# Closer lags in an attention pipeline that runs beside a weight stream: transposes five slots and values six behind the scores, rotations in halves, heads split two units ahead

## The chip, the cores and the metric

The kernel runs on one core of one Trainium2 chip. The metric is the device time of one execution in microseconds (us); where several runs are given, it is their median. Five engines work side by side, each with its own instruction list in a fixed order: TensorE (PE in the profile, its weight loads PEld), VectorE (DVE), ScalarE (ACT), GpSimd (POOL) and SyncE (SP, which here only issues DMAs). An instruction waits for semaphores of other engines, and everything behind it on its engine waits too.

## The reference, cut to what matters

One trunk layer for 512 tokens of width 2048, all in float32. An input projection feeds two mixers side by side, their outputs are normalised per group and projected back, and a SwiGLU block follows.

```
h = rmsnorm(x, g_mix)
qa, ka, va, qb, kb, vb = split(h @ w_in)            # 8 heads of q, 2 of k and v (A); 8 heads each (B)
# mixer A: grouped queries, all 512 keys
q = axial_rope(rmsnorm(qa, g_q)) * HD**-0.5;  k = axial_rope(rmsnorm(ka, g_k))
out_a = softmax(q @ k.T) @ va
# mixer B: three dilated windows (128,1), (512,4), (2048,16), merged by their softmax denominators
q = partial_rope(qb) * HD**-0.5;  k = partial_rope(kb)     # the first 32 of 128 dims are rotated
out_b = sum(wts * branch for branch in branches)
mixed = concat(rmsnorm(out_a, g_out_a), rmsnorm(out_b, g_out_b))
x = x + mixed @ w_out
gate, up = split(rmsnorm(x, g_ffn) @ w_gate_up)
x = x + (silu(gate) * up) @ w_down
out = rmsnorm(x, g_final)
```

## The kernel before

**Products.** Every float32 matrix product is made of three products of split operands: a value is divided into a high half (ACT writes it, rounded) and a low half (DVE subtracts the high half from the value). `split` (from L227) does this, `mm3` (L240 to L244) issues the three products hi x hi, hi x lo, lo x hi, so each full product shows as L242, L243, L244. The two lines of `split` without a gain are L233 (ACT) and L234 (DVE), with a gain L236 and L237.

**Units.** The weights stream in tiles of 128 rows. One `Unit` is one such tile with its 12 products (three for each of four row tiles of tokens, or of four column tiles). All units lie in one list, and the loop at the end of the program goes through it. The units that matter are those of the last input projections, then eight units for each of the four output chunks of mixer A, which start at unit 216 (`out_chunk("A", c)`), and from unit 248 the same for mixer B. An output chunk multiplies the eight heads' outputs with one 512-column block of W_out and adds the result, scaled per row, to x.

**Side work.** Attention is not a stage of its own: it is a list of small tasks (`side`) taken while units run. `give` (L711) adds credit: half of it after the second row tile of a unit (`by_rows`, L728), the rest at the unit's end; a task is taken while the credit covers its cost. Between `attend[0]` and `attend[1]` a unit brings 2.8 credits, from there to `attend[2]` 1.3 (`HEAD_RATE`), after that one credit per unit end. `attend[1]` lies `ATTEND_PAST` units behind the last input projection, `attend[2]` as many behind mixer A's output chunks. Where the program needs something not yet made, `drain_until` takes tasks at once, whatever their cost: for a head's output, and in `post` (the addition to x) for the row scale `ro`.

**Slots.** A task `head_slot(s)` (L643) issues, for four slots per head and sixteen heads (0 to 7 of A, 8 to 15 of B), one step of a pipeline: the score of slot s (three products on PE, then the maximum on DVE, L573, or for B the mask and maximum in one custom operation, L577), the normalisation of slot s-1 (L591, L592), the four transposes of probabilities of slot s-`TURN_LAG` (L597, then the split into `pTh` on ACT and `pTl` on DVE), the exponential on ACT (L584, L587), and the value products of slot s-`VALUE_LAG`. After a head's last value product `fin` copies its output (L614, `oT`) and squares it (L619); `add_squares` (L626) adds the squares of the heads into `acc`. After head 7 of a mixer `row_rms` goes to the front of the side list: PE's column sums of `acc` (L387), a copy and a scaling on DVE (L389, L222), a power on POOL (L224). The addition to x in `post` is L1022 on DVE. Behind it `h_side` (L1062) transposes x for the next stage (L1068).

**Other tasks between slots.** `norm_rope` rotates and normalises queries of A (L448 to L453 for one row tile). Its second block of queries (`qA1`) is loaded by a DMA and turned while the first heads run. `rope_partial` (L522, L525, L526) rotates a row tile of a projection `qkB`, that holds queries and keys of two heads of B; two row tiles are one task. `Back` loads and splits heads that were written to DRAM. `early(k)` splits the outputs of heads that stayed in SBUF (`oS`, L236 and L237 with `oT` as source), one unit before the unit that multiplies them.

**PSUM.** There are eight banks, handed out in the order in which they were released: four are held by the chunk, one by a head's output, three go round between scores, transposes of probabilities and transposes of queries and keys.

Of the kernel before, what the change touches and what calls it, by code (L numbers as in the profile page):

```python
# [15 lines left out]
OP = mybir.AluOpType  # L16
# [3 lines left out]
P = 128  # L20
# [3 lines left out]
NT = S // P  # L24
KD = D // P
NC = D // 512
NHA, NKV, NHB = 8, 2, 8
# [5 lines left out]
PARTIAL = HD // 4  # L33
# [21 lines left out]
EARLY = 2  # L55
EVICT = 6
HEAD_RATE = (2.8, 1.3)
TURN_LAG = 6
VALUE_LAG = 8
COLUMN_BLOCKS = 3  # L60
SUM_LEAD = 6
ATTEND_PAST = 6


def f32(ap):
# [4 lines left out]
def encoder_block(ctx, tc, x, g_mix, w_in, g_q_a, g_k_a, g_out_a, g_out_b, w_out, g_ffn,  # L70
                  w_gate_up, w_down, g_final, c_ident, c_mask, c_axial, c_partial, out):
    nc = tc.nc
# [13 lines left out]
    def slot(base, dtype=F32, shape=(P, 512)):  # L86
        return sp.tile(list(shape), dtype, tag="s", name=nm(base))
# [19 lines left out]
    def small(n=4):  # L107
        used[0] += n
        assert used[0] <= 512
        return smalls[:, used[0] - n:used[0]]  # L110
# [32 lines left out]
    turning = cp.tile([P, 512], F32, name="turning")  # L143
# [3 lines left out]
    ropeb = fixed[:, 256:512].rearrange("p (a t c) -> p a t c", a=2, t=NT)  # L147
# [72 lines left out]
    def rsqrt_mean(ss, n, count):  # L220
        t = small(n)
        nc.vector.tensor_scalar(t, ss, 1.0 / count, EPS, op0=OP.mult, op1=OP.add)  # L222
        r = small(n)
        nc.gpsimd.tensor_tensor(r, t, mhalf[:, :n], op=OP.pow)  # L224
        return r
# [23 lines left out]
    units = []  # L249
# [176 lines left out]
    def norm_rope(get, nh, name):  # L426
        w = nh * HD
        st = {}

        def squares(t):  # L430
            if t == 0:
                st["ss"] = small(NT * nh)
            junk, q0 = slot("rj"), get(t)[0]
            for h in range(nh):
                nc.scalar.activation(junk[:, h * HD:(h + 1) * HD], q0[:, h * HD:(h + 1) * HD], AF.Square,
                                     accum_out=st["ss"][:, nh * t + h:nh * t + h + 1])
            if t == NT - 1:
                st["rs"] = rsqrt_mean(st["ss"], NT * nh, HD)

        def turned(t):  # L440
            q0, dst = get(t)
            gc, gs = tabs[name]
            tmp = slot("ra")
            q4 = q0.rearrange("p (h a s d) -> p h a s d", h=nh, a=2, s=2)
            t4 = tmp[:, :w].rearrange("p (h a s d) -> p h a s d", h=nh, a=2, s=2)
            s4 = gs[:, t, :].rearrange("p (a s d) -> p a s d", a=2, s=2)
            for s in range(2):
                nc.vector.tensor_tensor(t4[:, :, :, s, :], q4[:, :, :, 1 - s, :],  # L448
                                        s4[:, None, :, s, :].to_broadcast([P, nh, 2, 32]), op=OP.mult)
            q3 = q0.rearrange("p (h d) -> p h d", h=nh)  # L450
            nc.vector.tensor_tensor(q3, q3, gc[:, t, :][:, None, :].to_broadcast([P, nh, HD]), op=OP.mult)
            nc.vector.tensor_tensor(q0, q0, tmp[:, :w], op=OP.add)
            nc.vector.tensor_tensor(dst.rearrange("p (h d) -> p h d", h=nh), q3,  # L453
                                    st["rs"][:, nh * t:nh * (t + 1), None].to_broadcast([P, nh, HD]), op=OP.mult)
        return [[lambda t=t, f=f: f(t) for t in range(NT)] for f in (squares, turned)]

    qA, kA, kTA, vA = {}, {}, {}, {}
    vB, qkB = {}, {}
# [20 lines left out]
    def reload(name, dst):  # L479
        assert stored[name] == NT, name  # L480
        whole = slot(name, F32, (P, NT, 512))
        nc.sync.dma_start(whole, spill[name].rearrange("t p c -> p t c"))
        dst.update((t, whole[:, t]) for t in range(NT))

    def split_vA(t):
        if not vA:
# [10 lines left out]
    def transpose_k_a(kv):  # L497
        ps = bank()
        for t in range(NT):
            nc.tensor.transpose(ps[:, t * P:(t + 1) * P], kA[t][:, 256 + kv * HD:256 + (kv + 1) * HD], ident)  # L500
        kTA[kv] = split(ps, "kT", at=((2, 4 + 2 * kv), (2, 5 + 2 * kv)))
        release(ps)
# [8 lines left out]
    def split_vB(h):  # L511
        vB[h] = split(vB[h].rearrange("p t c -> p (t c)"), "v", at=heads[NHA + h].home("v"))

    turn = [0]

    def rope_partial(q0, t):
        rot = q0.rearrange("p (h d) -> p h d", h=4)[:, :, :PARTIAL]
        turn[0] ^= 1
        tmp = turning[:, 256 + 128 * turn[0]:384 + 128 * turn[0]].rearrange("p (h c) -> p h c", h=4)
        hp = PARTIAL // 2  # L520
        for s in range(2):
            nc.vector.tensor_tensor(  # L522
                tmp[:, :, s * hp:(s + 1) * hp], rot[:, :, (1 - s) * hp:(2 - s) * hp],
                ropeb[:, 1, t, s * hp:(s + 1) * hp][:, None, :].to_broadcast([P, 4, hp]), op=OP.mult)
        nc.vector.tensor_tensor(rot, rot, ropeb[:, 0, t, :][:, None, :].to_broadcast([P, 4, PARTIAL]), op=OP.mult)  # L525
        nc.vector.tensor_tensor(rot, rot, tmp, op=OP.add)  # L526

    oT = {}
# [114 lines left out]
    def head_slot(s):  # L643
        def at(lag, f, only=None):
            head, i = head_at(s - lag)
            if head and (only is None or i == only):
                f(head, i)
        at(VALUE_LAG + 1, lambda head, i: head.add_squares(), NT - 1)
        at(0, Head.score)
        at(1, Head.norm)  # L650
        at(TURN_LAG, Head.pt)
        at(0, Head.exp)
        at(VALUE_LAG, Head.pv)
        at(VALUE_LAG, lambda head, i: head.fin(), NT - 1)
        at(-4, lambda head, i: head.tq(), 0)
# [6 lines left out]
    def light(cost, tasks):  # L662
        return [weighed(cost, f) for f in tasks]

    def attention_tasks():
        def q_tasks(j):
            return norm_rope(lambda t: (qA[j][t], qA[j][t]), 4, "q")

        def both(cost, *lists):
            return [weighed(cost, lambda fs=fs: [f() for f in fs]) for fs in zip(*lists)]  # L670

        def b_ropes(j):
            return light(0.5, [lambda t=t: (rope_partial(qkB[j][t], t), rope_partial(qkB[j][t + 1], t + 1))
                               for t in (0, 2)])
        qA.update({j: {} for j in range(2)})
        qkB.update({j: {} for j in range(4)})
        push_heads()
        k_squares, k_turned = norm_rope(lambda t: (kA[t][:, :256], kA[t][:, 256:]), NKV, "k")
        q_squares, q_turned = q_tasks(0)
        vs = [lambda t=t: split_vA(t) for t in range(NT)]  # L680
        tables = light(0.8, table_tasks())
        todo = tables[:3] + both(1.4, [lambda t=t: scale_k(t) for t in range(NT)], k_squares)
        todo += both(0.6, vs) + tables[3:]
        todo += both(2.0, q_squares, k_turned) + both(2.6, q_turned)
        todo += light(0.6, [lambda kv=kv: transpose_k_a(kv) for kv in range(NKV)]) + [heads[0].tq, heads[0].tk]
        extra = {}

        def at(slot, tasks):
            extra.setdefault(slot, []).extend(tasks)
        at(0, light(0.1, [lambda: reload("qA1", qA[1])]))  # L690
        at(20, light(0.1, [lambda: nc.sync.dma_start(mask, c_mask)]))
        for n, (cost, tasks) in enumerate(zip((1.0, 1.5), q_tasks(1))):
            for t, f in enumerate(both(cost, tasks)):
                at(3 + 4 * n + t, [f])
        for j in range(4):
            s = NT * (NHA + 2 * j)
            at(s - 11, light(0.1, [lambda j=j: reload(f"qkB{j}", qkB[j])]))
            for n, f in enumerate(b_ropes(j)):
                at(s - 8 + n, [f])
        for h in range(NHB):  # L700
            s = NT * (NHA + h)
            at(s + 2, light(0.1, [lambda h=h: load_vB(h)]))
            at(s + 4, light(0.4, [lambda h=h: split_vB(h)]))
        for s in range(2 * NHA * NT + VALUE_LAG + 2):
            cost = 1.5 if s < NHA * NT else 1.2 if s < 2 * NHA * NT else 0.7
            todo += [weighed(cost, lambda s=s: head_slot(s))] + extra.get(s, [])
        return todo
# [249 lines left out]
    todo = attention_tasks()  # L957
# [134 lines left out]
    for kind in "AB":  # L1092
        for c in range(NC):
            out_chunk(kind, c)
        if kind == "A":
            attend.append(len(units) + ATTEND_PAST)
    attend[1] += ATTEND_PAST

# [231 lines left out]
    at = [0.0]  # L1330
# [66 lines left out]
    for n, u in enumerate(units):  # L1397
        share["now"], share["due"] = n, 1.0
        if n < KD:
            if n + 5 < KD:  # L1400
                load_x(n + 5)
            if n + 1 < KD:
                x_prep(n + 1)
            if 4 < n < 10:
                next(gains, None)
        if n < KD + 8:
            row_squares(n)
        prepare(n)
        for v in units[n + 1:n + 2]:
            if v.early is not None:  # L1410
                v.early()
                v.early = None
        u.mm(u)
        if u.post is not None:
            u.post()
        for f in hooks.pop(n, ()):
            f()
        give(1.0)
# [54 lines left out]
```

## Time and profile before

| quantity | value |
|---|---|
| median of 3 runs | 1996.3 us (1996.21 to 1997.05) |
| the profiled execution | 1996.13 us |
| its span in the profile | 1994.3 us |
| mean granted TensorE clock | 0.996 |
| busy: PE, DVE, ACT, POOL | 99%, 80%, 57%, 6% |

A row of the timeline gives the start in the span, the duration, the engine, the line of the program, the operation with output<-input, and how many such instructions in a row it covers; in brackets stands the idle time of that engine just before and the engine, output and line that ended it. PE's products are pipelined: one starts some 0.23 us after the other, while each is listed with about 0.39. Names have their buffer numbers left out in the profile; the order of instructions has them. In the order, a row is one instruction (or `x4` alike) in the place that it has on its engine, without time.

### The profile page before, as it was taken

The numbers are of one execution on the slowest core, as the hardware profiler recorded it, in microseconds if no ns is written. First come the engines' busy times: TensorE is split into PE (matmuls) and PEld (weight loads), VectorE is DVE, ScalarE is ACT, GpSimd is POOL, SyncE is SP. The second block draws the span as 40 slices with busy tenths as digits, with TensorE's granted clock in tenths as the row PEclk, the third lists the DMA queues.
The fourth block names the chain that finished last, engine by engine and source line by source line (L and its number), as shares of the span: only waits on it lengthen the run. The fifth ranks groups of instructions, "written<-read, shape, count | busy, mean of one in ns | idle before, by whom it ended". The sixth has DMA issues, their size and how long they took to land. (4 is left out here: it accounts for less than half of the span.)

```text
span 1994.3 us, 27604 instructions
## 1 busy us (share of the span) xinstructions
PE 1971.8 (99%) x8972; PEld 1623.9 (81%) x8972; DVE 1594.9 (80%) x2773; ACT 1130.0 (57%) x2071; POOL 121.3 (6%) x162
## 2 busy tenths in 40 slices
PE   9999999999999999999999999999999999999998
PEld 7888888777888888888888888888888888788886
DVE  6887778887775698878878877878779887877977
ACT  7655555564555565554555555555556666666655
POOL 0100001000000000000000000000000122111121
PEclk9999999998999999999999999999999999999999
DMA  8576683143333644846737647558467698768765
GB/s 276 180 280 211 209 284 119 58 143 111 127 121 118 216 167 168 293 132 233 269 124 258 228 158 277 182 183 286 145 218 269 189 280 248 189 171 275 203 153 167
DMA packets 235874, 394.83 MB, mean 198 GB/s; under 512 B 22561, under 2 KB 77649, under 8 KB 235601
## 3 DMA queue, kind: packets, MB, share of 16 engines
q1 hardware_dynamic: 211440, 330.85, 49.1%
q0 software_dynamic: 17200, 40.38, 9.1%
q10 hardware_dynamic: 7088, 21.83, 3.1%
q8 instruction: 70, 1.15, 0.2%
q14 instruction: 76, 0.61, 0.1%
HBM read 330.33 MB, written 62.65 MB: 197 GB/s over the span
## 5 line engine op out<-in xcount | busy, mean ns | idle before, releaser
L242 PE MATMUL b<-tw,arena 128*128 128x512 f32 x2244 | 879.4, 392 | 2.4 <-ACT ev L1215 2.4
L243 PE MATMUL b<-tw,arena 128*128 128x512 f32 x2244 | 873.9, 389 | 0.8 <-DVE tw L830 0.4
L244 PE MATMUL b<-tw,arena 128*128 128x512 f32 x2244 | 874.1, 390 | 0.0
L827 ACT ACTIVATE tw<-raw 128x512 fp32r<-128x512 f32 x924 | 558.6, 628 | 430.3 <-DVE raw L871 276.5
L830 DVE TENSOR_TENSOR tw<-raw,tw 128x512 fp32r<-128x512 f32 x924 | 617.4, 685 | 167.7 <-ACT tw L827 161.4
L242 PEld LDWEIGHTS b<-tw,arena 128*128 128x128 f32 x2244 | 421.4, 188 | 89.3 <-ACT ev L1215 3.5
L243 PEld LDWEIGHTS b<-tw,arena 128*128 128x128 f32 x2244 | 421.5, 188 | 88.5 <-DVE tw L830 2.1
L244 PEld LDWEIGHTS b<-tw,arena 128*128 128x128 f32 x2244 | 421.2, 188 | 88.0
L871 DVE TENSOR_TENSOR raw<-raw,raw 128x512 f32<-128x512 f32 x528 | 360.0, 683 | 0.7 <-DMA raw<-in_w_gate_up_dram 0.6
L1216 POOL DMA_DIRECT2D x1d<-ev x76 | 66.5, 978 | 1146.8 <-ACT ev L1215 1136.7
L827 ACT ACTIVATE tw<-stage 128x512 fp32r<-128x512 f32 x140 | 85.4, 628 | 67.7 <-DVE stage L871 45.7
L830 DVE TENSOR_TENSOR tw<-stage,tw 128x512 fp32r<-128x512 f32 x140 | 93.3, 685 | 23.6 <-ACT tw L827 23.5
L242 PE MATMUL b<-w,arena 128*128 128x512 f32 x240 | 95.8, 399 | 0.0
L244 PE MATMUL b<-w,arena 128*128 128x512 f32 x240 | 93.9, 391 | 0.0
L233 ACT ACTIVATE pTh<-b 128x512 fp32r<-128x512 f32 x64 | 38.3, 599 | 97.7 <-PE b L597 94.6
L243 PE MATMUL b<-w,arena 128*128 128x512 f32 x240 | 93.5, 390 | 0.0
L365 DVE TENSOR_TENSOR pair<-pair 128x256 f32<-128x256 f32 x120 | 45.5, 420 | 26.7 <-ACT pair L1071 25.7
L1215 ACT ACTIVATE ev<-b,smalls 128x512 f32<-128x512 f32 x76 | 49.6, 682 | 27.5 <-PE b L244 26.2
L1119 DVE TENSOR_TENSOR s<-b,s 128x512 f32<-128x512 f32 x66 | 44.0, 687 | 24.8 <-PE b L244 24.8
L242 PE MATMUL b<-arena,arena 128*128 128x512 f32 x128 | 53.0, 414 | 2.0 <-ACT arena L236 2.0
L244 PE MATMUL b<-arena,arena 128*128 128x512 f32 x128 | 51.6, 403 | 2.0 <-DVE arena L237 2.0
L1147 ACT ACTIVATE pair<-b 128x512 f32<-128x512 f32 x44 | 26.3, 597 | 47.8 <-PE b L1144 47.5
(210 smaller groups left out, 1797.6 us busy)
## 6 DMA issues: line engine op xcount, KB each, us to landing
raw<-in_w_gate_up_dram SPq DMA_DIRECT2D x616, 256.0 KB, 5.3
raw<-in_w_down_dram SPq DMA_DIRECT2D x176, 256.0 KB, 7.0
stage<-in_w_in_dram SPq DMA_DIRECT2D x111, 256.0 KB, 5.0
forms<-pair SPq DMA_DIRECT2D x22, 896.0 KB, 5.3
x1d<-ev POOLq DMA_DIRECT2D x76, 256.0 KB, 6.7
fr<-forms ACTq DMA_DIRECT2D x35, 512.0 KB, 5.8
raw<-in_w_out_dram SPq DMA_DIRECT2D x32, 512.0 KB, 4.3
stage<-in_w_in_dram SPq DMA_DIRECT2D x90, 128.0 KB, 3.4
```

Source lines behind the costliest of these rows:

```text
L233: nc.scalar.activation(hi, src, AF.Copy)
L242: nc.tensor.matmul(dst, ah, bh, start=start, stop=False, skip_group_check=chained)
L243: nc.tensor.matmul(dst, ah, bl, start=False, stop=False, skip_group_check=chained)
L244: nc.tensor.matmul(dst, al, bh, start=False, stop=stop, skip_group_check=chained)
L365: nc.vector.tensor_tensor(out, x, y, op=op)
L827: nc.scalar.activation(self.pair[:, 0], self.src, AF.Copy)
L830: nc.vector.tensor_tensor(self.pair[:, 1], self.src, f32(self.pair[:, 0]), op=OP.subtract)
L871: nc.vector.tensor_tensor(t[dst], t[src[0]], t[src[1]], op=OP.add if form == "m6" else OP.subtract)
L1119: nc.vector.tensor_tensor(d[:, t], box.bank_of(form)[t], d[:, t], op=OP.add)
L1147: nc.scalar.activation(st["pair"][:, half * 1024:half * 1024 + 512], ps, AF.Copy)
L1215: nc.scalar.activation(e, box.bank_of(form)[t], AF.Copy, scale=r2["r"][:, row:row + 1])
L1216: nc.gpsimd.dma_start(x1_dram[2 * cb + j, row], e, accum_op=OP.add)
```

## The change

Six edits are made together. (1) `TURN_LAG` goes from 6 to 5 and `VALUE_LAG` from 8 to 6: transposes come five slots behind the score, the value products one slot behind the transposes in place of two; the list has two slots fewer at its end. (2) `ATTEND_PAST` goes from 6 to 4: `attend[2]` is unit 252 in place of 254, `attend[1]` 220 in place of 222. (3) `norm_rope` returns three lists: the addition of the rotated part and the scaling, until now the end of `turned`, are a task of their own, `scaled`. For the second block of queries the squares are at slots 0, 0, 1, 1, and the two halves alternate from slot 2 to 9; before, squares were at 3 to 6 and whole rotations at 7 to 10. (4) The reload of that block is the last task before slot 0 in place of the first behind it. (5) `rope_partial` rotates the four row tiles of a projection in one call of four operations, seven slots before the first head's score; before, there were two tasks of two calls, eight and seven slots ahead. (6) `early` is called for the next two units in place of the next one.

Three lines more in the program ahead of `norm_rope`'s end and fewer further down shift line numbers: L573 and L577 become L576 and L580, L591 and L592 become L594 and L595, L597 becomes L600, L626 becomes L629, L1022 becomes L1023, L1068 becomes L1069. L522, L525, L526 become L525, L528, L529.

```diff
-TURN_LAG = 6
-VALUE_LAG = 8
+TURN_LAG = 5
+VALUE_LAG = 6
...
-ATTEND_PAST = 6
+ATTEND_PAST = 4
...
             nc.vector.tensor_tensor(q3, q3, gc[:, t, :][:, None, :].to_broadcast([P, nh, HD]), op=OP.mult)
-            nc.vector.tensor_tensor(q0, q0, tmp[:, :w], op=OP.add)
+            st["tmp"] = tmp
+
+        def scaled(t):
+            q0, dst = get(t)
+            q3 = q0.rearrange("p (h d) -> p h d", h=nh)
+            nc.vector.tensor_tensor(q0, q0, st["tmp"][:, :w], op=OP.add)
             nc.vector.tensor_tensor(dst.rearrange("p (h d) -> p h d", h=nh), q3,
                                     st["rs"][:, nh * t:nh * (t + 1), None].to_broadcast([P, nh, HD]), op=OP.mult)
-        return [[lambda t=t, f=f: f(t) for t in range(NT)] for f in (squares, turned)]
+        return [[lambda t=t, f=f: f(t) for t in range(NT)] for f in (squares, turned, scaled)]
...
-    turn = [0]
-
-    def rope_partial(q0, t):
-        rot = q0.rearrange("p (h d) -> p h d", h=4)[:, :, :PARTIAL]
-        turn[0] ^= 1
-        tmp = turning[:, 256 + 128 * turn[0]:384 + 128 * turn[0]].rearrange("p (h c) -> p h c", h=4)
+    def rope_partial(q):
+        rot = q.rearrange("p t (h d) -> p t h d", h=4)[:, :, :, :PARTIAL]
+        tmp = turning.rearrange("p (t h c) -> p t h c", t=NT, h=4)
...
-        todo += both(2.0, q_squares, k_turned) + both(2.6, q_turned)
+        todo += both(2.0, q_squares, k_turned, k_scaled) + both(2.6, q_turned, q_scaled)
         todo += light(0.6, [lambda kv=kv: transpose_k_a(kv) for kv in range(NKV)]) + [heads[0].tq, heads[0].tk]
+        todo += light(0.1, [lambda: reload("qA1", qA[1])])
...
-        at(0, light(0.1, [lambda: reload("qA1", qA[1])]))
         at(20, light(0.1, [lambda: nc.sync.dma_start(mask, c_mask)]))
-        for n, (cost, tasks) in enumerate(zip((1.0, 1.5), q_tasks(1))):
-            for t, f in enumerate(both(cost, tasks)):
-                at(3 + 4 * n + t, [f])
+        q_squares, q_turned, q_scaled = q_tasks(1)
+        for t in range(NT):
+            at(t // 2, both(0.8, q_squares[t:t + 1]))
+            at(2 + 2 * t, both(0.9, q_turned[t:t + 1]))
+            at(3 + 2 * t, both(0.9, q_scaled[t:t + 1]))
         for j in range(4):
             s = NT * (NHA + 2 * j)
             at(s - 11, light(0.1, [lambda j=j: reload(f"qkB{j}", qkB[j])]))
-            for n, f in enumerate(b_ropes(j)):
-                at(s - 8 + n, [f])
+            at(s - 7, light(0.9, [lambda j=j: rope_partial(qkB[j]["whole"])]))
...
-        for v in units[n + 1:n + 2]:
+        for v in units[n + 1:n + 3]:
             if v.early is not None:
                 v.early()
                 v.early = None
```

More of the change, by code (lines that the diff above doesn't have):

```diff
@@ L483, in reload @@
         dst.update((t, whole[:, t]) for t in range(NT))
+        dst["whole"] = whole
     def split_vA(t):
@@ L522, in rope_partial @@
             nc.vector.tensor_tensor(
-                tmp[:, :, s * hp:(s + 1) * hp], rot[:, :, (1 - s) * hp:(2 - s) * hp],
-                ropeb[:, 1, t, s * hp:(s + 1) * hp][:, None, :].to_broadcast([P, 4, hp]), op=OP.mult)
-        nc.vector.tensor_tensor(rot, rot, ropeb[:, 0, t, :][:, None, :].to_broadcast([P, 4, PARTIAL]), op=OP.mult)
+                tmp[:, :, :, s * hp:(s + 1) * hp], rot[:, :, :, (1 - s) * hp:(2 - s) * hp],
+                ropeb[:, 1, :, s * hp:(s + 1) * hp][:, :, None, :].to_broadcast([P, NT, 4, hp]), op=OP.mult)
+        nc.vector.tensor_tensor(rot, rot, ropeb[:, 0][:, :, None, :].to_broadcast([P, NT, 4, PARTIAL]), op=OP.mult)
         nc.vector.tensor_tensor(rot, rot, tmp, op=OP.add)
@@ L670, in both @@
             return [weighed(cost, lambda fs=fs: [f() for f in fs]) for fs in zip(*lists)]
-        def b_ropes(j):
-            return light(0.5, [lambda t=t: (rope_partial(qkB[j][t], t), rope_partial(qkB[j][t + 1], t + 1))
-                               for t in (0, 2)])
         qA.update({j: {} for j in range(2)})
@@ L677, in attention_tasks @@
         push_heads()
-        k_squares, k_turned = norm_rope(lambda t: (kA[t][:, :256], kA[t][:, 256:]), NKV, "k")
-        q_squares, q_turned = q_tasks(0)
+        k_squares, k_turned, k_scaled = norm_rope(lambda t: (kA[t][:, :256], kA[t][:, 256:]), NKV, "k")
+        q_squares, q_turned, q_scaled = q_tasks(0)
         vs = [lambda t=t: split_vA(t) for t in range(NT)]
```

## The prediction, made before the changed kernel ran

> **What bounds the kernel now.** I read the page first: its busy row says where a change can act at all.
>
> ```profile
> PE 1971.8 (99%) x8972; PEld 1623.9 (81%) x8972; DVE 1594.9 (80%) x2773; ACT 1130.0 (57%) x2071; POOL 121.3 (6%) x162
> ```
>
> TensorE (PE) is busy for 1971.8 of the span's 1994.3 us, and the change leaves the number of its instructions as it was. So the time can fall only where PE waits or runs at a lower clock, and rises where a new wait appears. Next the list of waits, PE's rows: releaser, then us in total, times, the longest.
>
> ```profile
> PE b L597 <- DVE pTl L234: 3.0, 5, 1.5
> ...
> PE b L242 <- ACT arena L236: 2.0, 1, 2.0
> PE b L244 <- DVE arena L237: 2.0, 1, 2.0
> ...
> PE b L242 <- DVE smalls L577: 0.4, 1, 0.4
> ...
> PE b L244 <- DVE qTl L234: 0.2, 1, 0.2
> ```
>
> All five lie in the attention stage. Three belong to attention slots (pTl is the low half of transposed probabilities, smalls the sums of a masked score, qTl the low half of a query): 3.6 us in seven waits. The two arena rows belong to one place, where the projections end and the output product begins. PE's timeline there (start, duration, the wait before in brackets):
>
> ```profile
> 472.61 0.40 PE L244 MATMUL b<-arena,arena 128*128 128x512 f32 x1
> 475.01 0.50 PE L242 MATMUL b<-arena,arena 128*128 128x512 f32 x1 [2.00 <-ACT arena L236]
> ...
> 477.71 0.79 PE L244 MATMUL b<-arena,arena 128*128 128x512 f32 x1 [1.97 <-DVE arena L237]
> 478.31 1.70 PE L387 MATMUL b<-fixed,acc 128*128 128x1 f32 x8
> ...
> 486.25 0.40 PE L242 MATMUL b<-arena,arena 128*128 128x512 f32 x1
> ```
>
> Behind the two waits the products stay slow, so I asked for windows of 2 us (length, then busy time of PE, PEld, DVE, ACT and POOL; then the granted clock).
>
> ```profile
> 474.00:476.00 2.00, 0.73 (x2) 0.30 (x2) 1.90 (x8) 2.00 (x4) 0.00 (x0) 0.95 0.00 0
> 476.00:478.00 2.00, 0.29 (x1) 0.29 (x2) 1.62 (x4) 0.00 (x1) 0.00 (x0) 0.50 0.00 0
> ...
> 484.00:486.00 2.00, 2.00 (x7) 1.52 (x6) 1.39 (x3) 0.00 (x0) 0.00 (x0) 0.50 0.00 0
> 486.00:488.00 2.00, 2.00 (x13) 1.66 (x11) 0.98 (x3) 0.00 (x0) 0.00 (x0) 0.99 0.01 4
> ```
>
> The clock is halved from 476 to 486: the two waits cost their own length and then a stretch at half speed. For what this takes I need the pace at full clock, from a later place on PE's timeline, the end of mixer B's first output chunk:
>
> ```profile
> 623.32 0.95 PE L387 MATMUL b<-fixed,acc 128*128 128x1 f32 x8
> 624.13 0.49 PE L242 MATMUL b<-w,arena 128*128 128x512 f32 x1
> ...
> 626.99 0.39 PE L242 MATMUL b<-w,oSh 128*128 128x512 f32 x1
> ...
> 632.44 0.60 PE L1068 MATMUL b<-fixed,x 128*128 128x128 f32 x4
> ```
>
> From 626.99 to 632.44 stand 24 products: 0.227 us each. The eight sums of squares (L387) take 0.81 (623.32 to 624.13). Between 472.61 and 486.25 lie 19 products and L387: at full clock 19 x 0.227 + 0.81 = 5.1 us, in fact 13.6. **This transition loses 8.5 us**: some 4.4 by the waits, the rest by the half clock.
>
> **The transition, part by part.** The last products of mixer A's first output chunk need head 7's output, split into arena by ACT (L236) and then DVE (L237). ACT's and DVE's timelines show when:
>
> ```profile
> 470.04 0.58 ACT L614 ACTIVATE oT<-b 128x512 f32<-128x512 f32 x1
> ...
> 474.25 0.70 ACT L236 ACTIVATE arena<-oT,fixed 128x512 fp32r<-128x512 f32 x1
> ```
>
> ```profile
> 473.86 0.69 DVE L237 SCALAR_TENSOR_TENSOR arena<-b,arena 128x512 fp32r<-128x512 f32 x1 [0.23 <-ACT arena L236]
> ...
> 476.91 0.75 DVE L237 SCALAR_TENSOR_TENSOR arena<-oT,fixed,arena 128x512 fp32r<-128x512 f32 x1
> 480.04 0.16 DVE L389 COPY smalls<-b 128x4 f32<-128x4 f32 x1 [2.38 <-PE b L387]
> 480.24 0.17 DVE L222 TENSOR_SCALAR smalls<-smalls 128x4 f32<-128x4 f32 x1
> 481.57 0.75 DVE L1022 SCALAR_TENSOR_TENSOR x<-b,smalls,x 128x512 f32<-128x512 f32 x1 [1.16 <-POOL smalls L224]
> ```
>
> Head 7's output is there at 470.6, yet its low half is done only at 477.7, seven us later. What DVE does in between, in the order before (oT_4143 is head 7's output, qkB a projection being rotated):
>
> ```order
> L234 TENSOR_TENSOR pTl_4166<-b_75,pTh_4165 128x512
> L237 SCALAR_TENSOR_TENSOR arena_86<-b_77,arena_86 128x512
> L522 TENSOR_TENSOR turning<-qkB_287_4077,fixed 128x4x16 x2
> L525 TENSOR_TENSOR qkB_287_4077<-qkB_287_4077,fixed 128x4x32
> L526 TENSOR_TENSOR qkB_287_4077<-qkB_287_4077,turning 128x4x32
> L522 TENSOR_TENSOR turning<-qkB_287_4077,fixed 128x4x16 x2
> L525 TENSOR_TENSOR qkB_287_4077<-qkB_287_4077,fixed 128x4x32
> L526 TENSOR_TENSOR qkB_287_4077<-qkB_287_4077,turning 128x4x32
> L300 TENSOR_TENSOR arena_85<-raw_3705,arena_85 128x512
> L237 SCALAR_TENSOR_TENSOR arena_86<-oT_4143,fixed,arena_86 128x512
> ```
>
> and of the changed kernel, where head 7's output is oT_4075:
>
> ```order
> L594 RECIPROCAL smalls<-smalls 128x1
> L595 TENSOR_SCALAR p_4014<-p_4014,smalls 128x512
> L234 TENSOR_TENSOR pTl_4068<-b_73,pTh_4067 128x512
> L300 TENSOR_TENSOR arena_85<-raw_3572,arena_85 128x512
> L237 SCALAR_TENSOR_TENSOR arena_86<-oT_4075,fixed,arena_86 128x512
> L629 TENSOR_TENSOR acc_3118<-acc_3118,sq_4077 128x512
> ```
>
> The rotation and a query's split no longer stand before it, and the addition to acc has moved behind it. On PE, 21 products and 8 transposes (two groups) now stand between head 7's last value product and the first product that reads it, 21 x 0.227 plus 2 x 0.4 = 5.6 us. The chain is oT 0.58, ACT split 0.70, DVE split 0.75, about 2.0 by the rows above; with a pTl and an L300 of 0.68 ahead of it on DVE, 3.4. It is 2.2 us early. What was late next, at L387, had DVE's acc behind it: that is now one operation of 0.69 after the split, still ahead of the 12 products. So both waits go and, without them, the half clock: **-8.5 us**.
>
> **Lags, rotations and the partial rotation.** The seven slot waits come from DVE being busy with something long when a slot's pTl or sum is due. Rows of DVE, one query rotation (L448 to L453) and one call pair of the partial rotation (414.31 to 416.15, two such per projection):
>
> ```profile
> 354.84 0.76 DVE L448 TENSOR_TENSOR ra<-qA,gsq 128x256 f32<-128x256 f32 x2 [0.31 <-PE b L597]
> ...
> 357.08 0.69 DVE L453 TENSOR_TENSOR qA<-qA,smalls 128x512 f32<-128x512 f32 x1
> 357.69 0.68 DVE L573 TENSOR_REDUCE smalls<-b 128x1 f32<-128x512 f32 x1
> ...
> 414.31 0.35 DVE L522 TENSOR_TENSOR turning<-qkB,fixed 128x64 f32<-128x64 f32 x2
> ...
> 416.15 0.68 DVE L573 TENSOR_REDUCE smalls<-b 128x1 f32<-128x512 f32 x1
> ```
>
> A whole rotation holds DVE for 2.85 us (354.84 to 357.69); split, its halves hold it for about 1.5 and 1.3, one slot apart: the same instructions, no total saved. The merged partial rotation has four operations of the size of L448, L448, L451 and L452, so 2.24 us by the way from 354.84 to 357.08, in place of 2 x 1.84 = 3.68. It is bounded by 3.68 above, should its short runs of 16 and 32 elements go no faster in one call; below by 1.84, half the old work. I take 2.24, the row of equal size. DVE is not the bound, so the 1.4 us saved four times are worth only what they keep off a slot. How much room a slot has, from a plain slot and from the crowded one (PE, then DVE):
>
> ```profile
> 377.01 0.60 PE L597 MATMUL b<-fixed,p 128*128 128x128 f32 x4
> ...
> 380.56 0.48 PE L242 MATMUL b<-pTh,arena 128*128 128x512 f32 x1
> ...
> 422.98 0.66 PE L597 MATMUL b<-fixed,p 128*128 128x128 f32 x4 [1.49 <-DVE pTl L234]
> ...
> 453.08 0.66 PE L597 MATMUL b<-fixed,p 128*128 128x128 f32 x4 [0.23 <-DVE pTl L234]
> 456.33 0.60 PE L597 MATMUL b<-fixed,p 128*128 128x128 f32 x4
> ```
>
> ```profile
> 378.42 0.69 DVE L234 TENSOR_TENSOR pTl<-b,pTh 128x512 fp32r<-128x512 f32 x1
> ...
> 456.32 0.68 DVE L234 TENSOR_TENSOR pTl<-b,pTh 128x512 fp32r<-128x512 f32 x1
> ```
>
> With value products one slot behind the transposes in place of two, the transposes of 377.01 have their pTl at 379.11 and are read at 380.56: 1.45 us to spare. Those of 453.08 have it only at 457.00, behind the next transposes at 456.33: there the lag of one waits, unless DVE is relieved. Two rotation pairs lay on DVE just before; now one merged call stands seven slots ahead of a projection's use. I expect the seven waits to go with their restart, 0.16 us beyond each bracket (472.61 to 475.01 is 2.40, less a product 2.17, for a bracket of 2.00): 3.6 + 7 x 0.16 = **-4.7 us**. Against that, new waits of 0 to 0.5 us at the two slots behind a merged rotation, **+0.3**. The early reload of the second query block keeps its place on SP's queue, and ACT's splits of head outputs two units ahead are the same operations earlier: nothing, with ACT 57% busy as cover; without it a split costs PE at most its 0.70.
>
> **What the change adds.** Attention now ends its paced stretch at unit 252 rather than 254. Mixer B's row normalisation is then taken from the side list only when unit 255 drains it, and stands right ahead of the transposes that read its result. DVE in the order before (the end of mixer B's first output chunk):
>
> ```order
> L389 COPY smalls<-b_76 128x4
> L222 TENSOR_SCALAR smalls<-smalls 128x4
> L300 TENSOR_TENSOR w_5408<-raw_5174,w_5407 128x512
> L237 SCALAR_TENSOR_TENSOR oSl_5436<-oT_5383,fixed,oSh_5435 128x512
> L300 TENSOR_TENSOR w_5432<-raw_5174,w_5431 128x512
> L1022 SCALAR_TENSOR_TENSOR x_240_3763<-b_75,smalls,x_240_3763 128x512
> L1022 SCALAR_TENSOR_TENSOR x_241_3764<-b_71,smalls,x_241_3764 128x512
> ```
>
> and changed:
>
> ```order
> L300 TENSOR_TENSOR w_5360<-raw_5124,w_5359 128x512
> L300 TENSOR_TENSOR w_5381<-raw_5124,w_5380 128x512
> L389 COPY smalls<-b_72 128x4
> L222 TENSOR_SCALAR smalls<-smalls 128x4
> L1023 SCALAR_TENSOR_TENSOR x_242_3765<-b_71,smalls,x_242_3765 128x512
> L1023 SCALAR_TENSOR_TENSOR x_243_3766<-b_73,smalls,x_243_3766 128x512
> L1023 SCALAR_TENSOR_TENSOR x_244_3767<-b_77,smalls,x_244_3767 128x512
> L1023 SCALAR_TENSOR_TENSOR x_245_3768<-b_78,smalls,x_245_3768 128x512
> ```
>
> The work that stood between normalisation and addition has gone ahead of it. On PE, 36 products stood between L387 and the transposes of x (L1068); now 12 do. The chain's price, on DVE's timeline of before:
>
> ```profile
> 624.30 0.17 DVE L389 COPY smalls<-b 128x4 f32<-128x4 f32 x1 [2.71 <-PE b L387]
> ...
> 627.94 2.73 DVE L1022 SCALAR_TENSOR_TENSOR x<-b,smalls,x 128x512 f32<-128x512 f32 x4 [1.41 <-PE b L244]
> ```
>
> L387 to L389 is 0.98 (623.32 to 624.30). From L389 to the first addition, with only POOL's power between, 1.53 (480.04 to 481.57). Four additions take 2.73. The transposes read the last addition first or second, so they can go 0.98 + 1.53 + 2.73 = 5.2 us after L387. PE gets there after 0.81 + 12 x 0.227 = 3.5. The wait is 1.7, up to 2.1 if POOL is 0.4 slower than at 480; I take **+1.9**. Behind it on PE all later products queue. Nothing covers it.
>
> **Sum.** 1996.1 (the profiled execution; its span of 1994.3 and 1.8 around it; 0.2 below the median of 1996.3) - 8.5 - 4.7 + 0.3 + 1.9 = 1985.1; I say 1985.0.
>
> **The rivals.**
>
> *The half clock at the new wait.* If the 1.9 us wait drops the clock as the pair of 2.0 and 1.97 did, about 4.1 us come on top: 1989. For it: the trace halved the clock already in the window from 476, one gap and a half in. Against: the wait stands alone, and the 1.49 us wait at 422.98 was followed by no such stretch. The Trainium skill, page "TensorE: Matmul & The Clock Gate", Part 1, says the gate goes to half rate after an idle window of about 3.4 us that runs freely, and back after about as long a busy one; by that rule a single wait of 1.9 never trips it, which leaves 1985. The trace agrees on the half rate (0.50) but not on the way back: work was steady from 477.7, and 0.50 held until 486, 8 us. By the rule's 3.4 us the half clock would have cost some 1.7 instead of 4.1, and the sum would be near 1987.5. I go by the trace. Chance 0.10.
>
> *The transition keeps its wait.* If head 7's split is still late (a split two units ahead helps nothing when its input is late), 8.5 us stay: 1993.5. Against it stand the order rows and 2.2 us of room. Chance 0.08.
>
> *Slower: the lag of one starves PE.* At 453.08 a pTl took 3.92 us against 3.25 between transposes. Were DVE so late in most of the mixer B slots, with 0.5 to 0.7 us lost in each of 32, 16 to 22 us would come on top, 2001 to 2007. It decides once DVE's queue is over 1.45 us behind in a plain slot. Against: DVE works about 80% and idles between plain slots, so it catches up. Chance 0.07; a mild form of 4 to 7 us (1989 to 1992) 0.04.
>
> *No new wait.* If POOL and DVE pass the chain in 3.5 us: 1983. This lies inside my range; with the first case it makes 0.71.
>
> **How the numbers follow.** About 0.2% (4 us) is what a measurement of this kernel can tell from no change. Faster by more: the main case 0.71, the clock 0.10, the mild lag 0.04, less 0.01 at the edge: 0.84. Within: the kept wait and that edge, 0.09. Slower: 0.07. The range runs from 1982, with no new wait at all and a little more won at the slots, to 1990, which takes in the half clock; the kept wait and the starving lag, 0.15, stay outside, and part of the mild one.
>
> **What would show it.** Right: no arena wait at the transition, granted clock 1.0 there, hardly any pTl wait on PE, and one wait of about 1.9 on x (L1023) before L1069 near the end of mixer B's first chunk. Wrong: pTl waits at most value products, an arena wait on L237, or a window at 0.50 behind the new wait. The partial rotation is right if its four operations take about 2.2 us.

## The result, and the profile after

The changed kernel takes 1985.76 us (median of 4 runs, 1984.14 to 1988.21) against 1996.26 before; the ratio is 0.9948 with a 95% interval of 0.9931 to 0.9965. The forecast was 1985.0, faster, in a range of 1982 to 1990. The profiled execution took 1985.48, its span 1983.7, 10.6 less than before.

PE's waits after the change, from the list of waits (releaser, us in total, times, longest):

```profile
PE b L242 <- ACT ev L1216: 2.2, 2, 1.7
...
PE b L1069 <- DVE x L1023: 1.1, 2, 0.8
```

No row for pTl, smalls or qTl is left, and of arena only one of 0.4 us (for L336, in another stage), which stood in the list before too. One is new: PE waits for x, as the prediction's added step said. At the transition, PE, DVE and ACT:

```profile
460.27 0.40 PE L244 MATMUL b<-pTh,arena 128*128 128x512 f32 x1
...
466.21 0.40 PE L242 MATMUL b<-arena,arena 128*128 128x512 f32 x1
...
468.28 0.95 PE L387 MATMUL b<-fixed,acc 128*128 128x1 f32 x8
```

```profile
461.20 0.59 ACT L617 ACTIVATE oT<-b 128x512 f32<-128x512 f32 x1
...
462.67 0.73 ACT L236 ACTIVATE arena<-oT,fixed 128x512 fp32r<-128x512 f32 x1
```

```profile
463.44 0.75 DVE L237 SCALAR_TENSOR_TENSOR arena<-oT,fixed,arena 128x512 fp32r<-128x512 f32 x1 [1.38 <-ACT arena L236]
464.10 0.69 DVE L629 TENSOR_TENSOR acc<-acc,sq 128x512 f32<-128x512 f32 x1
```

Head 7's last value product starts at 460.27, its low half is done at 464.19, and PE reads it at 466.21. That is 2.0 us of room, where the prediction had 2.2. The clock, by windows of 2 us (the granted clock is the third number from the end), stays full:

```profile
466.00:468.00 2.00, 2.00 (x10) 1.65 (x9) 1.83 (x3) 1.25 (x4) 0.00 (x0) 1.00 0.97 304
468.00:470.00 2.00, 2.00 (x15) 1.74 (x15) 0.40 (x3) 0.00 (x0) 0.28 (x1) 1.00 1.06 398
```

The new wait, on PE's and then DVE's timeline:

```profile
616.03 0.95 PE L387 MATMUL b<-fixed,acc 128*128 128x1 f32 x8
...
619.48 0.39 PE L244 MATMUL b<-w,arena 128*128 128x512 f32 x1
620.67 0.33 PE L1069 MATMUL b<-fixed,x 128*128 128x128 f32 x1 [0.81 <-DVE x L1023]
621.33 0.55 PE L1069 MATMUL b<-fixed,x 128*128 128x128 f32 x3 [0.33 <-DVE x L1023]
621.64 0.47 PE L242 MATMUL b<-w,arena 128*128 128x512 f32 x1
```

```profile
617.02 0.17 DVE L389 COPY smalls<-b 128x4 f32<-128x4 f32 x1 [4.14 <-PE b L387]
...
618.55 2.73 DVE L1023 SCALAR_TENSOR_TENSOR x<-b,smalls,x 128x512 f32<-128x512 f32 x4 [1.16 <-POOL smalls L224]
```

Without a wait four transposes would start 0.23 after 619.48 and the next product 0.35 later, as at 632.44 and 632.79 before: at 620.06. It starts at 621.64, so the wait costs **1.6 us**, with no half clock behind it:

```profile
622.00:624.00 2.00, 2.00 (x10) 1.64 (x9) 0.69 (x1) 1.65 (x4) 0.00 (x0) 1.00 0.00 0
```

### The profile page after: what moved, and what is told of

It reads as the page before. It is cut to its first block, busy times and chain, and to the rows that moved or that the text cites. A ratio compares the mean times of both kernels' runs of the same rounds, so it can differ in the third digit from the quotient of the medians.

```text
span 1983.7 us, 27526 instructions
## 1 busy us (share of the span) xinstructions
PE 1968.0 (99%) x8972; PEld 1623.0 (82%) x8972; DVE 1589.3 (80%) x2725; ACT 1131.0 (57%) x2071; POOL 120.4 (6%) x162
## 4 chain that ended last, share of the span: by engine, by line
PE 94%; DVE 3%; ACT 1%; DMA 1%; issue 1%; ACTq 0%; POOL 0%; POOLq 0%; DVEq 0%; SPq 0%
PE b L242 30%; PE b L244 30%; PE b L243 30%; PE b L600 1%; PE b L1145 1%; DMA raw<-in_w_in_dram 1%; DVE raw L872 0%; DVE tw L831 0%; PE b L1069 0%; PE b L326 0%; PE b L550 0%; DVE arena L1196 0%; DVE w L300 0%; ACT rj L435 0%; DVE ra L448 0%
## 5 line engine op out<-in xcount | busy, mean ns | idle before, releaser
L831 DVE TENSOR_TENSOR tw<-raw,tw 128x512 fp32r<-128x512 f32 x924 | 618.8, 687 | 167.6 <-ACT tw L828 164.6
L831 DVE TENSOR_TENSOR tw<-stage,tw 128x512 fp32r<-128x512 f32 x140 | 93.6, 687 | 23.5 <-ACT tw L828 23.4
L244 PEld LDWEIGHTS b<-w,arena 128*128 128x128 f32 x240 | 45.0, 188 | 10.0
L243 PEld LDWEIGHTS b<-w,arena 128*128 128x128 f32 x240 | 45.2, 188 | 9.1
L242 PEld LDWEIGHTS b<-w,arena 128*128 128x128 f32 x240 | 45.1, 188 | 8.8
```

The costliest lines, as they stand in the source:

```text
L242: nc.tensor.matmul(dst, ah, bh, start=start, stop=False, skip_group_check=chained)
L243: nc.tensor.matmul(dst, ah, bl, start=False, stop=False, skip_group_check=chained)
L244: nc.tensor.matmul(dst, al, bh, start=False, stop=stop, skip_group_check=chained)
L831: nc.vector.tensor_tensor(self.pair[:, 1], self.src, f32(self.pair[:, 0]), op=OP.subtract)
```

## The experiments

Eleven kernels ran: four make one edit alone on the kernel before, seven undo a part of the changed kernel, move a cost in it or cut a task. Undoing the split two units ahead alone in the changed kernel was not tried, nor was the early reload by itself; it stays early in the runs with whole rotations. Each kernel has 4 to 10 runs that spread over 1 to 5 us, so a difference between two kernels of under some 3 us is read from their profiles, not from the medians alone.

| kernel | median us | ratio to before | 95% interval |
|---|---|---|---|
| split two units ahead alone | 1990.77 | 0.9975 | 0.9965 to 0.9986 |
| lags alone | 1989.94 | 0.9967 | 0.9957 to 0.9978 |
| paced stretch alone | 2000.61 | 1.0022 | 1.0013 to 1.0032 |
| merged rotation alone | 1990.64 | 0.9970 | 0.9959 to 0.9981 |
| changed, old paced stretch | 1985.42 | 0.9949 | 0.9935 to 0.9964 |
| changed, last slot cut | 1983.02 | 0.9934 | 0.9920 to 0.9949 |
| changed, rotation in pairs | 1987.72 | 0.9957 | 0.9940 to 0.9973 |
| changed, whole rotations at 10.0 credits | 1994.03 | 0.9987 | 0.9978 to 0.9996 |
| changed, whole rotations at 10.4 credits | 1987.64 | 0.9959 | 0.9944 to 0.9974 |
| changed, halves at 10.0 credits | 1994.66 | 0.9994 | 0.9985 to 1.0003 |
| changed, old lags | 1988.44 | 0.9961 | 0.9947 to 0.9975 |

### One edit alone

**Split two units ahead.**

```diff
-        for v in units[n + 1:n + 2]:
+        for v in units[n + 1:n + 3]:
```

> The kernel before with one edit: head outputs are split two units ahead. My theory: the transition's loss of 8.5 us is a matter of order alone. Head 7's split now stands on DVE right behind a pTl, ahead of the rotation, and PE has 15 products and 8 transposes (15 x 0.227 + 0.8 = 4.2 us) before it reads it, against a chain of 2.0 to 3.4. Both arena waits and the stretch at half clock go, the slot waits (4.7) stay: 1996.3 - 8.5 = 1987.8. Rival, the lags carry it (head 7's value products come two slots earlier by them, and without that its output is late whatever the split's place): the arena waits stay, 1996.

Measured 1990.77, 5.4 us gained of the 8.5. Both arena waits and the half clock are gone (1.00 in every window from 470 to 496), by the split's place alone. The rival falls. But with PE early, new small waits come up where DVE was still behind. Its PE timeline:

```profile
448.63 0.66 PE L597 MATMUL b<-fixed,p 128*128 128x128 f32 x4 [0.61 <-DVE smalls L577]
...
467.01 0.66 PE L597 MATMUL b<-fixed,p 128*128 128x128 f32 x4 [0.23 <-DVE pTl L234]
...
473.56 1.05 PE L387 MATMUL b<-fixed,acc 128*128 128x1 f32 x8 [0.20 <-DVE smalls L577]
...
486.08 0.50 PE L242 MATMUL b<-arena,arena 128*128 128x512 f32 x1 [0.35 <-DVE x L1022]
```

Their brackets are 1.4 us, some 2.0 with restarts. The profiled execution, the fastest of the eight, took 1989.66, which is 6.5 below the 1996.13 of before, so these waits account for what it lacks of 8.5. The median lies 1.1 above it, which they do not explain.

**Lags.**

```diff
-TURN_LAG = 6
-VALUE_LAG = 8
+TURN_LAG = 5
+VALUE_LAG = 6
```

> The kernel before with the lags of five and one slot alone; rotations whole, partial rotation in pairs, split one unit ahead. My theory: head 7's output is there two slots earlier, so the transition's 8.5 us go here too; whole rotations and rotation pairs leave the slot waits, and the crowded slots of mixer B lose 0.5 to 2 us more: 1988 to 1990. Rival, starvation: with one slot between transposes and value products and the old long rotations, most slots of mixer B wait 0.3 us or more: 1996 or over.

Measured 1989.94, no starvation. The crowded slot behind a rotation pair waits longer than before (2.10 in place of 1.49), and of the transition one wait remains, without a half clock:

```profile
425.78 0.66 PE L597 MATMUL b<-fixed,p 128*128 128x128 f32 x4 [2.10 <-DVE pTl L234]
...
477.48 0.50 PE L242 MATMUL b<-arena,arena 128*128 128x512 f32 x1 [1.20 <-ACT arena L236]
```

**The paced stretch.**

```diff
-ATTEND_PAST = 6
+ATTEND_PAST = 4
```

> The kernel before with the paced stretches ending two units earlier (220 and 252) alone. My theory: fewer tasks fall into the units around the transition, PE has 18 products between head 7's last value product and the first that reads it, and DVE has the split directly behind a pTl: the transition's 8.5 us go, 1987.8, with 36 products before the transposes of x at mixer B's first chunk and no wait there. Rival, the lags carry it: arena waits stay, 1996.

Measured 2000.61: **slower by 4.4, and my theory was wrong.** PE, then ACT:

```profile
475.08 0.64 PE L242 MATMUL b<-arena,arena 128*128 128x512 f32 x1 [2.56 <-ACT arena L236]
...
489.87 0.50 PE L242 MATMUL b<-arena 128*128 128x512 f32 x1 [1.66 <-DVE pTl L234]
...
492.98 1.11 PE L597 MATMUL b<-fixed,p 128*128 128x128 f32 x4 [2.14 <-DVE x L1022]
```

```profile
472.64 0.72 ACT L587 ACTIVATE p<-p,smalls 128x512 f32<-128x512 f32 x1 [0.88 <-DVE smalls L577]
...
473.36 0.58 ACT L614 ACTIVATE oT<-b 128x512 f32<-128x512 f32 x1
...
474.31 0.72 ACT L236 ACTIVATE arena<-oT,fixed 128x512 fp32r<-128x512 f32 x1
```

With less credit ahead of the transition, head 7's last slots are drained one unit before they are needed, with no weight product between some of them. My 18 products stood ahead of L387, not ahead of the first reader of head 7: there were three. On ACT the output's copy stands behind an exponential that itself waits for DVE. Two stretches at half clock follow, from 475.3 and from 492.4. The split two units ahead asks for the slots a unit earlier and so may be what keeps this edit harmless in the changed kernel; no run tests that, and the next section shows that the edit gains nothing there.

**The merged rotation.** The diff is that of `rope_partial` and its task in the change above.

> The kernel before with the partial rotation over four row tiles in one call alone. My theory: the four operations take about 2.2 us per projection in place of 3.7; of the slot waits those behind rotation pairs in mixer B go (1.49, 0.40 and 0.23 with their restarts, 2.6 us). At the transition the rotation no longer stands ahead of head 7's low half, but a split of values and a projection's split do: the first arena wait of 2.0 stays, the second shrinks to about 0.7, so 1.3 us more: 1992.4. If the clock then no longer halves, 4.1 more: 1988.3. Rival, short runs of 16 and 32 elements cost as much in one call: 3.7 us per projection, 1995 to 1996.

Measured 1990.64, between the two cases that I named. In brackets, 1.49 became 0.78 and 0.40 and 0.23 became 0.24; at the transition 1.97 became 0.20, and the half clock is shorter. PE's timeline, and a window:

```profile
475.39 0.50 PE L242 MATMUL b<-arena,arena 128*128 128x512 f32 x1 [2.04 <-ACT arena L236]
476.32 0.50 PE L244 MATMUL b<-arena,arena 128*128 128x512 f32 x1 [0.20 <-DVE arena L237]
```

```profile
478.00:480.00 2.00, 2.00 (x6) 1.54 (x6) 0.77 (x2) 0.00 (x0) 1.03 (x1) 0.50 0.00 0
```

Three edits, each alone, win 5.4, 6.3 and 5.6 us, together more than the whole change does: they remove largely the same loss, the transition's. The merged rotation also moves the credits (0.9 per projection in place of twice 0.5), and no run separates that from its shorter work.

### Parts undone in the changed kernel

**The old paced stretch.**

```diff
-ATTEND_PAST = 4
+ATTEND_PAST = 6
```

> The changed kernel with the paced stretches ending at 222 and 254 again. My theory: mixer B's row normalisation then stands 54 products ahead of the transposes of x in place of 12, so the two waits on x (1.14 us in brackets, 1.7 by PE's starts) go and nothing else comes: 1984. Rival, the earlier end is needed against the transition's wait: about 1.2 us of it comes back, as with the lags alone, and the sum is 1985.5, no change.

Measured 1985.42 (1984.52 to 1989.29), inconclusive by time. By its profile the wait on x is gone, and only a slot wait of 0.15 is new in the attention stage; the transition has no wait, so the rival's number came without its reason. Between 1674 and 1688, though, PE waits three times for tw (L831), 1.3 us in brackets and 1.8 with restarts, which the changed kernel does not: about what the wait on x cost. Its span is 1982.5.

**The last slot cut.**

```diff
-        for s in range(2 * NHA * NT + VALUE_LAG + 2):
+        for s in range(2 * NHA * NT + VALUE_LAG + 1):
```

> The changed kernel without the last attention slot of the list, which issues nothing but costs 0.7 credit; the row normalisation of mixer B is then taken one unit earlier, 24 products ahead of the transposes of x in place of 12. My theory: 24 products and the column sums are 6.3 us, more than the chain of 5.2: the waits on x go, 1.7 us less, 1984. Rival, POOL's and DVE's chain is not the cause and the wait moves along with the normalisation: no change, 1985.8.

Measured 1983.02 (1982.19 to 1984.37), 2.7 below the changed kernel; the two intervals against before overlap. By the profiles the span is 1.9 shorter, and the wait on x is 1.6 of that. PE's timeline shows the cause of the wait settled:

```profile
613.31 0.95 PE L387 MATMUL b<-fixed,acc 128*128 128x1 f32 x8
...
619.70 0.60 PE L1069 MATMUL b<-fixed,x 128*128 128x128 f32 x4
```

6.39 us and 24 products lie between, no wait in them. The removed slot issued nothing (8972 instructions on PE in both profiles), so no work is left out. It is the version with the lowest median here.

**The rotation in pairs.** `rope_partial` and its two tasks as before, in the changed kernel.

> The changed kernel with the partial rotation in pairs of row tiles again, two tasks per projection. My theory: with a lag of one slot the two slots behind a rotation pair wait for pTl, about 2.1 at one and 0.2 to 0.5 at two others as with the lags alone, with restarts about +3 us: 1988.8. The transition stays without a wait. Rival, the merged rotation is worth nothing once lags and splits are changed: 1985.8.

Measured 1987.72, 2.0 more: three waits of 0.54, 0.26 and 0.23 come back near 450, 1.5 us with restarts. They are read from a profiled execution of 1991.19, the slowest of the four, which also has a half clock at 1709. The 2.1 of the lags alone did not come. The pairs cost 0.1 credit more per projection than the merged call, so this run moves the slots too; which of the two held the long wait off was not tested.

**Whole rotations.** `norm_rope` with two lists and its tasks at slots 3 to 10, as before.

> The changed kernel with whole rotations of the second query block again (slots 7 to 10). My theory: one to three waits of about 0.46 for pTl come back while the rotations run, 0.6 to 1.9 us with restarts: 1986.4 to 1987.7. Rival, the halves matter to the time nothing, since transposes now come a slot earlier: 1985.8.

Measured 1994.03, 8.3 more and far outside both expectations. Next to the 0.47 that I expected, there are three larger waits on PE, none of them at a rotation of queries:

```profile
424.60 0.66 PE L595 MATMUL b<-fixed,p 128*128 128x128 f32 x4 [1.38 <-DVE pTl L234]
453.88 0.50 PE L242 MATMUL b<-kTh,qTh 128*128 128x512 f32 x1 [1.02 <-DVE smalls L575]
518.45 0.79 PE L242 MATMUL b<-arena 128*128 128x512 f32 x1 [2.58 <-DVE arena L234]
```

The first two follow a merged partial rotation. DVE's timeline ahead of the first:

```profile
420.20 0.69 DVE L524 TENSOR_TENSOR qkB<-qkB,turning 128x512 f32<-128x512 f32 x1
420.81 0.68 DVE L300 TENSOR_TENSOR arena<-raw,arena 128x512 fp32r<-128x512 f32 x1
421.41 0.74 DVE L997 SCALAR_TENSOR_TENSOR arena<-oback,fixed,arena 128x512 fp32r<-128x512 f32 x1
...
423.86 0.68 DVE L234 TENSOR_TENSOR pTl<-b,pTh 128x512 fp32r<-128x512 f32 x1
```

In the changed kernel the two splits (L300 and the one of `oback`) stand ahead of that rotation, and its pTl starts at 422.63, with no wait. ACT's timeline ahead of the third:

```profile
515.89 0.60 ACT L233 ACTIVATE pTh<-b 128x512 fp32r<-128x512 f32 x1 [5.67 <-DMA oB<-oT]
```

By its bracket ACT sat 5.67 us until a transfer had read an earlier head's output; I take it that pTh needed that buffer. Squares and rotations had cost 10.4 credits with halves (four at 0.8, eight at 0.9), and 10.0 whole (four at 1.0, four at 1.5). So I formed a new theory, that 0.4 credits did it, and crossed the two.

Whole rotations, credits as in the changed kernel (the diff is against the run before this one):

```diff
-        for n, (cost, tasks) in enumerate(zip((1.0, 1.5), q_tasks(1))):
+        for n, (cost, tasks) in enumerate(zip((1.0, 1.6), q_tasks(1))):
```

> The changed kernel with whole rotations (slots 7 to 10) at a cost of 1.6 in place of 1.5 each, so that rotations and squares cost 10.4 credits as in the changed kernel and not 10.0; from slot 10 on PE's order is that of the changed kernel, instruction for instruction. My theory now: what the whole rotations cost in the run with them at 10.0 (8.3 us) came nearly all from the 0.4 credits, which shift every later slot against the weight units, and not from the rotations: one wait of about 0.5 near 370 us stays, those at 425, 454 and 518 go: 1986.4. Rival, the whole rotations leave DVE late for the rest of the stage: the waits stay, 1992 to 1994.

Halves, credits as with whole rotations:

```diff
-            at(2 + 2 * t, both(0.9, q_turned[t:t + 1]))
+            at(2 + 2 * t, both(0.8, q_turned[t:t + 1]))
```

> The changed kernel with the first halves costing 0.8 credits in place of 0.9, so that rotations and squares cost 10.0; from slot 10 on PE's order is that of the run with whole rotations at 10.0. My theory: the 0.4 credits alone bring back the waits of 1.4 near 424, 1.0 near 454 and 2.6 near 518 with a stretch at half clock, without the one near 372: 1992 to 1993.5. Rival, the halves themselves carried the gain: no change, 1985.8.

Measured 1987.64 and 1994.66. PE's timeline of the first, then of the second:

```profile
372.70 0.66 PE L595 MATMUL b<-fixed,p 128*128 128x128 f32 x4 [1.27 <-DVE pTl L234]
```

```profile
425.71 0.66 PE L600 MATMUL b<-fixed,p 128*128 128x128 f32 x4 [1.38 <-DVE pTl L234]
...
454.89 0.50 PE L242 MATMUL b<-kTh,qTh 128*128 128x512 f32 x1 [0.96 <-DVE smalls L580]
...
519.49 0.50 PE L242 MATMUL b<-arena 128*128 128x512 f32 x1 [2.64 <-DVE arena L234]
```

The theory holds both ways, though each run is 1.2 us slower than I gave: the wait near 372 is longer than 0.5, the second run has one of 0.69 more at 352.41, and no half clock. A cost of 0.1 less on four tasks, with the same instructions, costs 8.9 us. The halves themselves are worth 1.9 by the medians; the ranges of the two kernels overlap, and the one wait of 1.27 that comes back makes 1.4 with its restart.

**The old lags.**

```diff
-TURN_LAG = 5
-VALUE_LAG = 6
+TURN_LAG = 6
+VALUE_LAG = 8
```

> The changed kernel with the lags of six and two slots again. My theory: the split two units ahead protects the transition, and mixer B's normalisation stands 36 products ahead of its readers, so the waits on x go (1.7 us). But with the paced stretch ended at 220, two slots of the last heads of A are drained with no product between them; DVE's 1.80 us per slot of B against PE's 1.84 leave no room there, and one or two waits of up to 1 us come: 1984.5 to 1986.5. Rival, the lags are what the gain rests on: the arena wait and the half clock are back, 1992 or more.

Measured 1988.44, 2.7 above the changed kernel and 2 above what I gave. The transition keeps no wait, so the rival falls; slots wait 1.05 near 354, 0.28 near 454, 0.55 and 0.24 near 463. The first of them is far from the drained slots that I had named.

## Why the prediction was right, step by step

**The transition (-8.5): right, mechanism and size.** Up to the end of unit 255 PE is 12.9 us ahead of before (629.71 less 0.81, where before had already paid its column sums, against 616.03), and the prediction's two terms with the 0.3 give 12.9. That is their sum; the run with the split two units ahead alone gives this term by itself, 6.5 won in its profiled execution and 2.0 of new waits. Which edit does it was left open in the prediction, and the runs show that more than one does: the split two units ahead removes it all alone, the lags all but 1.2.

**The slot waits (-4.7, +0.3): right in sum, in part by luck.** All seven are gone, and no new one of up to 0.5 came at the merged rotations. The four operations of one, on DVE's timeline, with the next instruction:

```profile
418.72 0.76 DVE L525 TENSOR_TENSOR turning<-qkB,fixed 128x256 f32<-128x256 f32 x2
419.51 0.69 DVE L528 TENSOR_TENSOR qkB<-qkB,fixed 128x512 f32<-128x512 f32 x1
420.23 0.69 DVE L529 TENSOR_TENSOR qkB<-qkB,turning 128x512 f32<-128x512 f32 x1
420.84 0.68 DVE L629 TENSOR_TENSOR acc<-acc,sq 128x512 f32<-128x512 f32 x1
```

2.12 us, for a forecast of 2.24 and 3.68 before. The reason, though, was half the story. The prediction named long DVE work as the cause and wrote of the halves "no total saved". The crossed pair shows that the credits of the new tasks, which no step priced, hold 8.9 us: they decide where each later slot falls against the weight products and against the transfers that free its buffers. For the transition and the new wait the prediction read the changed kernel's own order, in which these costs are contained. For the slots it showed no such rows. Its reason for the longest wait, that a merged call relieves DVE, does not carry it: that wait is absent with rotations in pairs too, and it is back, at 1.38, behind a merged rotation once the credits are 0.4 lower. That the slots of the changed kernel fall well is luck as far as the prediction's working goes.

**The new wait (+1.9): right place, 0.3 too large.** L387 to L389 took 0.99 and L389 to the first addition 1.53, as forecast, and the last addition ends 5.25 after L387, for a forecast of 5.2. The prediction's own difference was 1.7; the 0.2 that it added for a slower POOL was not needed, and PE came to the transposes after 3.68 us, not 3.5. The run with the last slot cut shows by undoing it that the distance in products was the cause.

**The rival of the half clock at this wait** did not come, in any of the five profiles that have this wait. But it came where nobody looked, 1080 us later, behind a wait that the change does not touch. PE's timeline and a window after, then the same place before:

```profile
1703.93 0.79 PE L242 MATMUL b<-tw,arena 128*128 128x512 f32 x1 [1.68 <-ACT ev L1216]
```

```profile
1704.00:1706.00 2.00, 2.00 (x5) 1.62 (x6) 1.98 (x4) 2.00 (x4) 1.71 (x2) 0.50 0.99 352
```

```profile
1715.70 0.50 PE L242 MATMUL b<-tw,arena 128*128 128x512 f32 x1 [1.68 <-ACT ev L1215]
```

```profile
1716.00:1718.00 2.00, 2.00 (x10) 1.62 (x9) 1.97 (x4) 2.00 (x4) 1.75 (x2) 1.00 0.91 324
```

Ahead of it PE had gained 11.8 us (1715.70 against 1703.93), at the end 10.6. So this stretch takes back about 1.1 of them. It may also be why runs of the changed kernel spread over 4 us; that is argued, not shown.

**The sum.** The profiled execution came within 0.4 us of the forecast's 1985.1, and part of this is luck: the half clock at 1704 took 1.1, while the new wait was 0.3 cheaper than forecast and a wait of 0.38 at 1698.19 before (DVE tw L830, 0.5 with its restart), of which the prediction says nothing, is gone.

**The slower rival, starvation by the lag of one,** fell with the lags alone (1989.94).

## What to carry to other kernels

On engines that issue in order, count the instructions that stand between a result's last input and its first reader, turn them into time by the pace of that engine, and hold them against the producer's chain: here 5.6 us against 3.4 and 3.5 against 5.2 gave both large terms within 0.3 us. Where side work is paced by cost numbers, these are part of the schedule: change a cost only with the resulting order in hand, and when a part is undone for a test, keep the sum of the costs, or the test measures the shift. Edits that remove the same wait don't add up.

## What the runs showed of the hardware

The length of a single wait does not decide whether the clock halves. Nearly the same wait at the same place, 2.58 and 2.64 near 519, was followed by half clock with whole rotations at 10.0 credits and by full clock with halves at 10.0:

```profile
518.00:520.00 2.00, 1.55 (x4) 1.16 (x5) 2.00 (x4) 0.19 (x1) 0.00 (x0) 0.56 0.93 278
```

```profile
520.00:522.00 2.00, 2.00 (x12) 1.64 (x12) 2.00 (x6) 0.60 (x2) 0.00 (x0) 1.00 1.02 376
```

The unchanged wait of 1.66 to 1.68 near 1710 halved it in 3 of 13 profiles (the changed kernel, the one with paired rotations, the one with old lags). Windows of 0.1 us show such a stretch to last 3.41 us (1704.0 to 1707.4), and so do the six other single ones in these profiles; the one before the change lasted three times that (475.8 to 486.0). In the run of the paced stretch alone two of them start at 475.29 and 492.35, five times 3.41 apart. The Trainium skill, page "TensorE: Matmul & The Clock Gate", Part 1, has the window run freely, about 3.4 us long. That fits the lengths, the distance and the dependence on chance; its condition of a whole idle window does not fit, as a wait of 1.68 was enough. The prediction saw no agreement on the way back to full clock. Counted in windows of 3.41 from 475.8 there is one: the windows end at 479.2, 482.6 and 486.0, the products run on without a gap only from 479.87, behind the column sums, so the third window is the first that they fill, and the clock is full right behind it.
